# A hybrid layer on one Trainium2 core: the memory rows' sum of squares, computed at another place in the program

## Chip, cores and metric

One core of a Trainium2 chip runs the whole kernel. The metric is device time in microseconds (us) of one execution; the time of a kernel is the median of its runs. Engines are named as in the profile: PE (TensorE matmuls), PEld (its weight loads), DVE (VectorE), ACT (ScalarE), POOL (GpSimd) and SP (SyncE, which here only issues DMAs).

## What is computed

One layer on 256 tokens of width 2048 in float32: a projection to 7,440 columns, a gated delta rule (8 heads) and an RWKV7 recurrence (16 heads) on its parts, an output projection, a cross attention to 256 memory rows, and a squared-ReLU MLP of hidden width 8192. The part that the change touches is the norm of the memory:

```python
def rmsnorm(x, w):
    xf = x.astype(jnp.float32)
    y = xf * lax.rsqrt(jnp.mean(xf * xf, axis=-1, keepdims=True) + RMS_EPS)
    return (y * w.astype(jnp.float32)).astype(x.dtype)
...
    k = (mn @ wk).reshape(b, m, XA_HEADS, XA_HEAD_DIM)
    v = (mn @ wv).reshape(b, m, XA_HEADS, XA_HEAD_DIM)
```

Here mn is rmsnorm(mem). The reciprocal root of each memory row (one number per row, the tile `rm`) is a factor that can be applied behind the matmul, so `rm` is first needed when the projection wk has been accumulated.

## The kernel before

All large products run as split float32: a weight block of 512 KB (`raw`, 128 x 1024) comes in by a DMA of the SP queue, ACT casts a half of it to a high part (`whi`, L239), DVE subtracts to get the low part (`wlo`, L110), and PE runs six matmuls of 512 columns on each half: high by high (L254), high by low (L255), low by high (L257), for two blocks of rows. There are four buffers of `raw` and three each of `whi` and `wlo`. A GEMM of one group of 512 columns takes eight blocks, here called blocks 1 to 8, each with halves a and b.

The input projection is read group by group, `win_group` (L784). The RWKV part takes, for u = 0 to 3, a group with r and k (`rk_group`, L799), for even u a group with v (`v_group`, L804), and then `unit(u)` (L810), the recurrence of four heads. The accumulated group is scaled into two tiles `pt` (128 x 512) of the pool `ptp`, which has four buffers and is also where squares of rows are computed. The delta rule follows (`dn_in`, `dn_unit`), then two groups for its gate (`z_group`), then the memory's projections wk and wv. Each unit inverts a triangular matrix in `inverse` (L481): it writes the matrix to memory (L488), reads the diagonal blocks back as `g16` (L490), works on them with DVE, and goes through memory once more (L519, L521). These four DMAs are issued by ACT.

The sum of squares of the memory rows is `rms_dram` (L292). Eight times, SP issues a load of 128 x 512 of `mem` into a tile `junk` of that pool (L297), and ACT squares it in place and accumulates the row sums (L122, called from L298). DVE then adds the eight sums (L300, L287) and POOL takes the power -0.5 (`rm`, L289). In the kernel before, it is called at L1018, behind `dn_unit(1)` and ahead of the two gate groups.

The program's order is not the order of the code: a scheduler puts each engine's instructions into one list, weight loads and casts first (`high_priority`, L212 and L230), and a list is executed in order. It also decides which buffer of the pool a `junk` tile gets, and so what its load has to wait for.

Of the kernel before, what the change touches and what calls it, by code (L numbers as in the profile page):

```python
# [17 lines left out]
P = 128  # L18
# [86 lines left out]
def body(ctx, tc, I, out, dbg=None, upto=99):  # L105
# [14 lines left out]
    def act(o, a, f, scale=1.0, bias=0.0, accum=None):  # L120
        kw = {} if accum is None else {"accum_out": accum}
        return A.activation(o, a, f, bias=bias, scale=scale, **kw)  # L122
# [16 lines left out]
    def nm(s):  # L139
        cnt[0] += 1  # L140
        return f"{s}_{cnt[0]}"
# [144 lines left out]
    def rms_end(ss, name):  # L286
        ts(ss, ss, 1.0 / D, ALU.mult, EPS, ALU.add)  # L287
        r = const.tile([P, 2], F32, name=name)
        power(r, ss, -0.5, 2)  # L289
        return r  # L290

    def rms_dram(src, name):  # L292
        part = small.tile([P, 2, 4], F32, tag="ssp", name=nm("ssp"))
        for m in range(2):
            for q in range(4):
                junk = ptp.tile([P, 512], F32, tag="pt", name=nm("junk"))
                nc.sync.dma_start(out=junk, in_=src[:, m, 512 * q:512 * (q + 1)])  # L297
                act(junk, junk, AF.Square, accum=part[:, m, q:q + 1])  # L298
        ss = small.tile([P, 2], F32, tag="ss", name=nm("ss"))
        V.tensor_reduce(ss, part, axis=AX.X, op=ALU.add)  # L300
        return rms_end(ss, name)
# [497 lines left out]
    def rk_group(u):  # L799
        pt = win_group()  # L800
        stream[0] = 2
        return rw_shift(pt, 0, ("r", "k"), (2 * u, 2 * u + 1))

    def v_group(u):  # L804
        pt = win_group()
        stream[0] = 2
        for i in range(2):
            vs[u + i] = rw_shift(pt, 256 * i, ("v",), (2 * (u + i), 2 * (u + i) + 1))[0]

    def unit(u, rk_):  # L810
        stream[0] = u % 2
        rw_unit(u, rk_[0], rk_[1], vs[u])

    for u in range(4):
        t = rk_group(u)
        if u % 2 == 0:
            v_group(u)
        unit(u, t)
        if upto <= 1:
            return  # L820
    rps.close()
# [193 lines left out]
    Vm = late.tile([P, 2, NB], F32, name="Vm")  # L1015
    obs = [dn_unit(0, *kqv)]
    obs.append(dn_unit(1, *dn_in(1)))
    rm = rms_dram(I["mem"].rearrange("(m p) d -> p m d", p=P), "rm")  # L1018
    z_group(0)
    z_group(1)  # L1020
    stream[0] = 2
# [217 lines left out]
```

## Time and profile before

| what | value |
|---|---|
| median of 3 runs | 1428.85 us (1423.86 to 1430.27) |
| the profiled execution's own time | 1427.91 us |
| its span, first to last instruction | 1426.2 us |
| PE busy | 1407.6 us, 99% of the span |
| DVE, ACT, POOL busy | 945.7, 776.2, 53.0 us |
| mean granted clock of TensorE | 0.995 |
| DMA traffic | 250.80 MB, 176 GB/s over the span |

The profile is of one execution. Busy time is the time in which an engine had an instruction in work; the row of a wait names the instruction that began late and what came last of the things it waited for. A number in brackets at the end of a timeline row is idle time of that engine ahead of the row. [...]

### The profile page before, as it was taken

The numbers are of one execution on the slowest core, as the hardware profiler recorded it, in microseconds if no ns is written. First come the engines' busy times: TensorE is split into PE (matmuls) and PEld (weight loads), VectorE is DVE, ScalarE is ACT, GpSimd is POOL, SyncE is SP. The second block draws the span as 40 slices with busy tenths as digits, with TensorE's granted clock in tenths as the row PEclk, the third lists the DMA queues.
The fourth block names the chain that finished last, engine by engine and source line by source line (L and its number), as shares of the span: only waits on it lengthen the run. The fifth ranks groups of instructions, "written<-read, shape, count | busy, mean of one in ns | idle before, by whom it ended". The sixth has DMA issues, their size and how long they took to land.

```text
span 1426.2 us, 22860 instructions
## 1 busy us (share of the span) xinstructions
PE 1407.6 (99%) x8308; PEld 1172.1 (82%) x8308; DVE 945.7 (66%) x1788; ACT 776.2 (54%) x1476; POOL 53.0 (4%) x66
## 2 busy tenths in 40 slices
PE   9999999999999999999999999999999999999997
PEld 7877888788887878888788888888888888888886
DVE  7748563858688685766776555665556665566664
ACT  7655554455556454556765544555445544455553
POOL 0010001010010000000000000000000000000000
PEclk9999999999999999999999999999999999999999
DMA  7444443454358455555465566555665556655564
GB/s 272 160 154 142 137 130 106 136 195 140 105 186 238 141 170 173 177 177 178 140 200 189 187 191 198 186 187 192 192 193 191 189 188 194 194 185 188 192 192 148
DMA packets 90114, 250.80 MB, mean 176 GB/s; under 512 B 20609, under 2 KB 29329, under 8 KB 89617
## 3 DMA queue, kind: packets, MB, share of 16 engines
q1 hardware_dynamic: 69728, 241.86, 52.3%
q10 hardware_dynamic: 19920, 6.42, 1.9%
q8 instruction: 65, 1.06, 0.3%
q0 software_dynamic: 352, 1.06, 0.2%
q14 instruction: 49, 0.39, 0.1%
HBM read 242.62 MB, written 6.69 MB: 175 GB/s over the span
## 4 chain that ended last, share of the span: by engine, by line
PE 51%; issue 0%; ACT 0%; DVE 0%; POOLq 0%; POOL 0%
PE ps_g L278 17%; PE ps_g L281 9%; PE ps_g L255 8%; PE ps_g L254 8%; PE ps_g L257 8%; PE ps_g L223 0%; PE ps_g L225 0%; PE ps_g L224 0%; PE ps_x L320 0%; PE ps_s L320 0%; PE ps_s L1112 0%; ACT h L122 0%; ACT junk L122 0%; ACT whi L239 0%; POOLq L1235 0%
## 5 line engine op out<-in xcount | busy, mean ns | idle before, releaser
L110 DVE TENSOR_TENSOR wlo<-raw,whi 128x512 fp32r<-128x512 f32 x848 | 582.1, 691 | 366.6 <-ACT whi L239 314.2
L239 ACT CAST whi<-raw 128x512 fp32r<-128x512 f32 x848 | 524.0, 621 | 485.7 <-DVE wlo L110 202.6
L278 PE MATMUL ps_g<-hhl,whi 128*128 128x512 f32 x1088 | 297.3, 395 | 0.0
L254 PE MATMUL ps_g<-whi,xhl 128*128 128x512 f32 x512 | 207.4, 405 | 0.9 <-ACT whi L239 0.6
L278 PEld LDWEIGHTS ps_g<-hhl,whi 128*128 128x128 f32 x1088 | 186.7, 189 | 25.5
L255 PE MATMUL ps_g<-whi,xhl 128*128 128x512 f32 x512 | 204.1, 399 | 0.0
L254 PE MATMUL ps_g<-whi,fhi 128*128 128x512 f32 x480 | 186.8, 389 | 0.0
L255 PE MATMUL ps_g<-whi,flo 128*128 128x512 f32 x480 | 186.8, 389 | 0.0
L281 PEld LDWEIGHTS ps_g<-hhl,wlo 128*128 128x128 f32 x1088 | 166.3, 189 | 22.6
L281 PE MATMUL ps_g<-hhl,wlo 128*128 128x256 f32 x1088 | 172.9, 281 | 0.0
L257 PE MATMUL ps_g<-wlo,xhl 128*128 128x512 f32 x512 | 170.4, 405 | 2.1 <-DVE wlo L110 2.1
L257 PE MATMUL ps_g<-wlo,fhi 128*128 128x512 f32 x480 | 151.5, 389 | 0.0
L254 PEld LDWEIGHTS ps_g<-whi,xhl 128*128 128x128 f32 x512 | 97.2, 190 | 23.6 <-issue 1.7
L255 PEld LDWEIGHTS ps_g<-whi,xhl 128*128 128x128 f32 x512 | 97.1, 190 | 21.1 <-issue 2.2
L257 PEld LDWEIGHTS ps_g<-wlo,xhl 128*128 128x128 f32 x512 | 94.3, 190 | 23.8 <-DVE wlo L110 4.5
L255 PEld LDWEIGHTS ps_g<-whi,flo 128*128 128x128 f32 x480 | 90.1, 188 | 18.8
L257 PEld LDWEIGHTS ps_g<-wlo,fhi 128*128 128x128 f32 x480 | 90.1, 188 | 18.7
L254 PEld LDWEIGHTS ps_g<-whi,fhi 128*128 128x128 f32 x480 | 90.1, 188 | 18.5
L113 DVE SCALAR_TENSOR_TENSOR cy<-ps_x,colt,cy 128x255 f32<-128x255 f32 (+2 forms) x72 | 34.2, 475 | 2.8 <-ACT cy L122 2.1
L1205 ACT CAST fhi<-hid 128x256 fp32r<-128x256 f32 x64 | 26.1, 407 | 9.7 <-DVE hid L113 9.4
L113 DVE SCALAR_TENSOR_TENSOR h<-ps_g,rf,h 128x512 f32<-128x512 f32 (+1 forms) x34 | 22.9, 716 | 12.0 <-PE ps_g L225 8.7
L113 DVE SCALAR_TENSOR_TENSOR hid<-hid 128x256 f32<-128x256 f32 x64 | 27.3, 427 | 2.1
(353 smaller groups left out, 1440.2 us busy)
## 6 DMA issues: line engine op xcount, KB each, us to landing
raw<-in_w_dram SPq DMA_DIRECT2D x256, 512.0 KB, 4.2
raw<-in_w_in_dram SPq DMA_DIRECT2D x112, 512.0 KB, 3.5
raw<-in_w_out_dram SPq DMA_DIRECT2D x32, 512.0 KB, 4.3
raw<-in_wk_dram SPq DMA_DIRECT2D x8, 512.0 KB, 3.8
raw<-in_wv_dram SPq DMA_DIRECT2D x8, 512.0 KB, 3.5
raw<-in_wq_dram SPq DMA_DIRECT2D x8, 512.0 KB, 3.8
raw<-in_wo_dram SPq DMA_DIRECT2D x8, 512.0 KB, 3.5
wl<-in_w_lora_dram SPq DMA_DIRECT2D x8, 272.0 KB, 6.3
```

The costliest lines, as they stand in the source:

```text
L110: return (e or V).tensor_tensor(o, a, b, op=op)
L113: return V.scalar_tensor_tensor(o, a, s, b, op0=op0, op1=op1)
L239: A.copy(hi, w)
L254: T.matmul(acc[m][:, :n], lhsT=xh, rhs=w[q][0], start=first, stop=False)
L255: T.matmul(acc[m][:, :n], lhsT=xl, rhs=w[q][0], start=False, stop=False)
L257: T.matmul(acc[m][:, :n], lhsT=lhs(kb * KB + q, m)[0], rhs=w[q][1], start=False, stop=last)
L278: T.matmul(acc, lhsT=w[k][0], rhs=rhs(8 * b + k).rearrange("p a t -> p (a t)"), start=b == 0 and k == 0, stop=False)
L281: T.matmul(acc[:, 0:S], lhsT=w[k][1], rhs=rhs(8 * b + k)[:, 0], start=False, stop=b == 1 and k == 7)
L1205: A.copy(hi[:, j], t)
```

## The change

The call of `rms_dram` moves from L1018 to the loop over the RWKV units, behind `unit(1)`. Nothing else is edited.

```diff
@@ -816,6 +816,8 @@
         if u % 2 == 0:
             v_group(u)
         unit(u, t)
+        if u == 1:
+            rm = rms_dram(I["mem"].rearrange("(m p) d -> p m d", p=P), "rm")
         if upto <= 1:
             return
     rps.close()
@@ -1015,7 +1017,6 @@
     Vm = late.tile([P, 2, NB], F32, name="Vm")
     obs = [dn_unit(0, *kqv)]
     obs.append(dn_unit(1, *dn_in(1)))
-    rm = rms_dram(I["mem"].rearrange("(m p) d -> p m d", p=P), "rm")
     z_group(0)
     z_group(1)
     stream[0] = 2
```

What the scheduler makes of it, first on the SP queue, which issues the loads. In the kernel before, the eight loads of the memory (`junk`, numbers 1019 to 1026) stand among the weight loads of the first gate group (its blocks 4 to 8):

```order
L232 DMA raw_1047_5268<-in_w_in_dram 128x1024
L297 DMA junk_1019_5169<-in_mem_dram 128x512
L297 DMA junk_1020_5172<-in_mem_dram 128x512
L232 DMA raw_1052_5290<-in_w_in_dram 128x1024
L297 DMA junk_1021_5175<-in_mem_dram 128x512
L297 DMA junk_1022_5178<-in_mem_dram 128x512
L232 DMA raw_1057_5312<-in_w_in_dram 128x1024
L297 DMA junk_1023_5181<-in_mem_dram 128x512
L232 DMA raw_1062_5334<-in_w_in_dram 128x1024
L297 DMA junk_1024_5184<-in_mem_dram 128x512
```

Now they stand in the fourth group of the input projection, r and k of unit 2 (below: group 4), whose blocks 1 to 8 are `raw_340` to `raw_375` by the first number. The first row is its block 5:

```order
L232 DMA raw_360_1908<-in_w_in_dram 128x1024
L297 DMA junk_327_1787<-in_mem_dram 128x512
L297 DMA junk_328_1790<-in_mem_dram 128x512
L297 DMA junk_329_1793<-in_mem_dram 128x512
L232 DMA raw_365_1930<-in_w_in_dram 128x1024
L297 DMA junk_330_1796<-in_mem_dram 128x512
L232 DMA raw_370_1952<-in_w_in_dram 128x1024
L297 DMA junk_331_1799<-in_mem_dram 128x512
L297 DMA junk_332_1802<-in_mem_dram 128x512
L297 DMA junk_333_1805<-in_mem_dram 128x512
L232 DMA raw_375_1974<-in_w_in_dram 128x1024
L297 DMA junk_334_1808<-in_mem_dram 128x512
```

So all eight loads now go past the loads of blocks 6 to 8 and of the next group. The third to sixth wait, by their semaphores, for the square of the one two places ahead (329 for 327, 330 for 328, 331 for 329, 332 for 330); the seventh and eighth wait for PE's transposes of the `pt` tiles of unit 1.

Second, ACT in group 4, from the cast of half 2b to that of 4b. Before (2b is `whi_338`, 3a `whi_341`, 4b `whi_348`):

```order
L239 CAST whi_338_1818<-raw_335_1812 128x512
L122 ACTIVATE sh_r_255_1381<-ps_x_254_1376,der_81 128x256
L239 CAST whi_341_1836<-raw_340_1834 128x512
L239 CAST whi_343_1840<-raw_340_1834 128x512
L122 ACTIVATE sh_r_255_1381<-ps_x_254_1376,der_81 128x256
L239 CAST whi_346_1858<-raw_345_1856 128x512
L239 CAST whi_348_1862<-raw_345_1856 128x512
```

Now (2b is `whi_348`, 3a `whi_351`, 4b `whi_358`):

```order
L239 CAST whi_348_1848<-raw_345_1842 128x512
L122 ACTIVATE junk_327_1787,ssp_326_1786<-junk_327_1787 128x512
L122 ACTIVATE sh_r_255_1381<-ps_x_254_1376,der_81 128x256
L239 CAST whi_351_1866<-raw_350_1864 128x512
L122 ACTIVATE junk_328_1790,ssp_326_1786<-junk_328_1790 128x512
L239 CAST whi_353_1870<-raw_350_1864 128x512
L122 ACTIVATE sh_r_255_1381<-ps_x_254_1376,der_81 128x256
L239 CAST whi_356_1888<-raw_355_1886 128x512
L122 ACTIVATE junk_329_1793,ssp_326_1786<-junk_329_1793 128x512
L239 CAST whi_358_1892<-raw_355_1886 128x512
```

A square of the memory now stands ahead of the casts of 3a, 3b and 4b, and each square is behind the landing of its load.

Third, ACT around halves 6a and 6b of the same group. Before (6a is `whi_356`, 6b `whi_358`):

```order
L239 CAST whi_353_1884<-raw_350_1878 128x512
L122 ACTIVATE sh_k_257_1391<-ps_x_256_1386,der_81 128x256
L519 DMA inv0_83<-x16_175_935 64x256
L239 CAST whi_356_1902<-raw_355_1900 128x512
L122 ACTIVATE sh_k_257_1391<-ps_x_256_1386,der_81 128x256
L122 ACTIVATE kk_267_1423<-sh_k_257_1391,der_81 128x256
L122 ACTIVATE th_270_1427<-sh_k_257_1391,colt_75 128x256
L239 CAST whi_358_1906<-raw_355_1900 128x512
```

Now (6a is `whi_366`, 6b `whi_368`):

```order
L239 CAST whi_363_1914<-raw_360_1908 128x512
L122 ACTIVATE sh_k_257_1391<-ps_x_256_1386,der_81 128x256
L122 ACTIVATE junk_331_1799,ssp_326_1786<-junk_331_1799 128x512
L519 DMA inv0_83<-x16_175_935 64x256
L239 CAST whi_366_1932<-raw_365_1930 128x512
L122 ACTIVATE junk_332_1802,ssp_326_1786<-junk_332_1802 128x512
L122 ACTIVATE junk_333_1805,ssp_326_1786<-junk_333_1805 128x512
L122 ACTIVATE sh_k_257_1391<-ps_x_256_1386,der_81 128x256
L122 ACTIVATE kk_267_1423<-sh_k_257_1391,der_81 128x256
L122 ACTIVATE th_270_1427<-sh_k_257_1391,colt_75 128x256
L239 CAST whi_368_1936<-raw_365_1930 128x512
```

One square now stands ahead of the cast of 6a, and two more ahead of that of 6b. From group 4 on, up to the memory's projections, the small work of the units also stands elsewhere among the matmuls, by a few places.

## Rows read from the trace of the kernel before

**Rows 1.** The page: busy time by engine, and the chain that ended last.

```profile
PE 1407.6 (99%) x8308; PEld 1172.1 (82%) x8308; DVE 945.7 (66%) x1788; ACT 776.2 (54%) x1476; POOL 53.0 (4%) x66
...
PE 51%; issue 0%; ACT 0%; DVE 0%; POOLq 0%; POOL 0%
```

**Rows 2.** What PE waited for, whole span (total us, times, longest), its second entry.

```profile
PE ps_s L673 <- DVE IP L113: 1.5, 1, 1.5
```

**Rows 3.** Stretches: length, busy PE, PEld, DVE, ACT, POOL (instructions), granted clock, DMA share, GB/s.

```profile
250.00:300.00 50.00, 48.07 (x394) 36.44 (x392) 35.20 (x78) 26.85 (x57) 6.90 (x9) 0.93 0.39 127
...
450.00:500.00 50.00, 49.15 (x436) 38.86 (x435) 36.70 (x87) 27.14 (x52) 5.37 (x3) 0.97 0.51 157
...
272.00:276.00 4.00, 2.49 (x71) 1.68 (x70) 4.00 (x11) 1.24 (x2) 0.00 (x0) 1.00 0.10 25
```

**Rows 4.** The tile junk: durations in ns (min/median/max), starts, waits, time to landing.

```profile
L297 SPq DMA_DIRECT2D junk<-in_mem_dram x8: 328/328/454, 422.4 to 441.3; - x8
L122 ACT ACTIVATE junk<-junk x8: 627/632/634, 428.0 to 445.9; 128x512 f32<-128x512 f32 x8
...
  DMA junk<-in_mem_dram: 4.8, 4
...
DMA to landing us min/median/max: 4.2/4.4/5.1
```

**Rows 5.** What PE waited for between 415 and 455 us.

```profile
PE ps_g L257 <- DVE wlo L110: 1.9, 3, 1.0
```

**Rows 6.** Timelines of ACT, DVE and PE between 427 and 439 us.

```profile
427.97 0.63 ACT L122 ACTIVATE junk<-junk 128x512 f32<-128x512 f32 x1
...
428.60 0.60 ACT L239 CAST whi<-raw 128x512 fp32r<-128x512 f32 x1
...
430.42 0.68 ACTq L490 DMA_DIRECT2D g<-scr  x1
...
437.02 0.17 DVE L117 TENSOR_SCALAR x<-g 64x8 f32<-64x8 f32 x1 [2.83 <-DMA g<-scr]
...
438.44 0.73 PE L257 MATMUL ps_g<-wlo,xhl 128*128 128x512 f32 x2 [1.03 <-DVE wlo L110]
```

**Rows 7.** DMA issues: queue, count, KB each, median us to landing.

```profile
out_dram<-h SPq DMA_DIRECT2D x4, 256.0 KB, 2.9
...
g<-scr ACTq DMA_DIRECT2D x6, 64.0 KB, 3.1
```

**Rows 8.** Timelines of SP and ACT in group 4, 108 to 124 us.

```profile
108.53 0.33 SPq L232 DMA_DIRECT2D raw<-in_w_in_dram  x1
...
111.11 0.62 ACT L239 CAST whi<-raw 128x512 fp32r<-128x512 f32 x1 [2.08 <-PE ps_g L255]
112.01 0.47 ACT L122 ACTIVATE sh_r<-ps_x,der 128x256 f32<-128x256 f32 x1 [0.28 <-PE ps_x L320]
112.38 1.18 ACT L239 CAST whi<-raw 128x512 fp32r<-128x512 f32 x2
...
121.08 0.49 ACTq L519 DMA_DIRECT2D inv<-x  x1
...
122.22 0.47 ACT L122 ACTIVATE sh_k<-ps_x,der 128x256 f32<-128x256 f32 x1
...
123.39 1.13 ACT L239 CAST whi<-raw 128x512 fp32r<-128x512 f32 x2
```

**Rows 9.** Timeline of PE in group 4: the first matmul of halves 3a, 4b, 6a and 6b.

```profile
114.55 0.39 PE L254 MATMUL ps_g<-whi,xhl 128*128 128x512 f32 x1
...
119.19 0.40 PE L254 MATMUL ps_g<-whi,xhl 128*128 128x512 f32 x1
...
123.31 0.39 PE L254 MATMUL ps_g<-whi,xhl 128*128 128x512 f32 x1
...
124.81 0.48 PE L254 MATMUL ps_g<-whi,xhl 128*128 128x512 f32 x1
```

**Rows 10.** What PE waited for between 100 and 160 us.

```profile
PE ps_g L254 <- DVE pt L117: 0.3, 1, 0.3
```

## The prediction

> **What bounds the kernel now.** Read the page's first part and its chain first [rows 1]: PE is busy 1407.6 of 1426.2 us, and the chain that ended last is, where an engine is named at all, PE. DVE (66%) and ACT (54%) have room on the average. So an edit that leaves the matmuls as they are can win only what PE does not use: its waits, and time at the lower clock. Next come the waits of PE over the whole span and the granted clock by stretches [rows 2, 3]. The largest single wait behind the start is 1.5 us; the clock was below 1.00 in two places only: 0.93 over the stretch 250 to 300 and 0.97 over 450 to 500, that is 0.07 x 50 + 0.03 x 50 = 5.0 us of full-speed time lost. Everything that lies on the table is therefore a few us of 1428, and the question is whether the moved step gives or takes such a few us.
>
> **What the step costs where it stands now.** The view of the tile junk [rows 4] shows eight loads of 256 KB issued from 422.4 to 441.3, landing after 4.2 to 5.1 us (median 4.4), and eight squares; ACT stood still 4.8 us in four of them, waiting for the data. PE's waits in that stretch are 1.9 us in three [rows 5]. The longest, 1.03 us at 438.44, can be followed in the timelines [rows 6]: ACT issued the read of the diagonal blocks (g from scr) at 430.42, DVE got it at 437.02 after 2.83 us of standing still, and the low half that PE wanted stood behind it in DVE's list. So this read took 6.6 us, where the median of its six is 3.1 [rows 7]; it ran while the memory's loads did. I count 1.0 us as the step's price there. The other two waits (0.9 us together) are of low halves too; nothing in the rows ties them to the memory, so they are worth between 0 and 0.9. **Given back: 1.0 us, bounds 0 and 1.9.**
>
> **What it costs where it goes.** The work is the same: eight loads, eight squares, two small DVE operations, one POOL operation. A square takes 0.63 us of ACT's list (427.97 to 428.60, [rows 6]), eight of them 5.0. What matters is what stands behind them. In group 4 ACT's casts feed PE with three buffers of high halves, so a cast that is late by more than its lead stops PE. I walk the new lists with the times of the old group 4 [rows 8, 9] and the median landing of 4.4.
>
> Half 3a: the load of block 5 was issued at 108.53; the first memory load follows 0.33 later, 108.9, and lands at 113.3. ACT has finished the cast of 2b at 111.7 and stands. Square until 113.9, the shift sh_r (0.37, from 112.01 to 112.38) until 114.3, then the cast of 3a, 0.62, done at 114.9. PE took up 3a at 114.55. **PE late by 0.4.**
>
> Half 4b: the third load waits for the first square, 114.0, and lands at 118.4; square, cast, done at 119.6. PE was at 4b at 119.19, now 119.6. **Nothing more.** The second square goes into the gap behind the cast of 3a (to 115.5), so the fourth load goes out at 115.5 and lands at 119.9, its square is done at 120.5.
>
> Half 6a: the fifth load waits for the third square, 119.0, lands at 123.4, square to 124.0; ACT issues the DMA L519 (0.49), cast from 124.5, done at 125.1. PE was at 6a at 123.31, with the 0.4 at 123.7. **Late by 1.4.**
>
> Half 6b: the sixth load waits for the fourth square, 120.5, lands at 124.9, the seventh just behind it. Behind the cast of 6a (next start 125.05) come two squares to 126.3, then sh_k, kk and th, 1.17 us as before (122.22 to 123.39), then the cast of 6b, done at 128.1. PE needs it 1.5 us behind 6a (123.31 to 124.81), at 126.6. **Late by 1.5.**
>
> Sum 0.4 + 1.4 + 1.5 = **3.3 us**. With the longest landing of rows 4, 5.1 us, three landings follow each other up to 6a, and the same walk gives 1.1 + 0.7 + 2.1 + 1.5 = 5.4. With the shortest landing for a transfer of this size on this queue, 2.9 us (the output's stores, [rows 7]), only the two squares ahead of 6b are felt, 0.5 us. I take 4.4, because it was measured on these very loads among the same weight loads; 0.5 and 5.4 stay as the ends. The 0.3 us that PE already waited in this part [rows 10] are left as they are.
>
> [...]
>
> **What else moves.** The weight loads that now stand behind memory loads on SP: block 6 is issued behind the third memory load (114.4) and needed by the cast of 6a at 121 or later, so it has 6 us; block 8 is issued behind the seventh (about 121.5) and needed some 6 us behind 6a. Both are covered by a landing of about 4.4 to 5; if that goes to 6, block 8 is late by little. POOL: rm now stands ahead of the eight masks of the next scores, and waits for the last square. That is done before 130; the masks follow matmuls that begin later than that, so I put it at nothing; if a square came 2 us later, the masks would be late by that, off PE's path as long as DVE's inversion has lead. DVE's two small sums (0.15 us each in their place) are nothing beside PE. At the memory's projections rm is simply there.
>
> **The sum.** 3.3 - 1.0 = +2.3 on the profiled execution's own 1427.91 us (span 1426.2, the rest around it): **1430.2 us**. That execution lies 0.9 below the median of the runs shown, 1428.85, so the change against the median is +1.4 to +2.3, a tenth or two of a per cent. 0.5%, about what a measurement of this kernel can tell from no change, is 7.1 us: faster means below 1421.7, slower above 1436.0. I expect no change.
>
> **Rivals.**
>
> *The loads land early.* With 2.9 us instead of 4.4 the cost is 0.5 and the gain stays: 1427.91 + 0.5 - 1.0 = 1427.4. For it: at this place the DMA engines have less to do than between 422 and 446. Against it: here too the weights stream on the same queue, and four of the old squares waited for their data.
>
> *The moved order removes clock falls.* The lower clock at 276 to 288 came just behind a stretch in which PE was busy 2.49 of 4 us [rows 3], among the many tiny matmuls of an inversion, and behind the 1.5 us wait of rows 2. The small work now stands at other places. If both falls (5.0), that wait (1.5) and all of 1.9 us go, and the new place costs 0.5, the sum is -7.9: 1420.0, faster. For it: nothing ties these falls to a fixed place. Against it: six inversions remain, each with its runs of tiny matmuls.
>
> *The new waits bring the lower clock (slower).* Place: halves 6a and 6b of group 4. There PE would stand 2.9 us within 5, or 3.6 with the long landing, as sparse as the 2.49 of 4 us that came ahead of the fall at 276. Price: 5.4 of waits, nothing given back, and a fall such as the one at 276, 0.07 x 50 = 3.5 us: 1427.91 + 8.9 = 1436.8. It decides if the landings are above 5 us and a fall follows; with only one of the two the sum stays within 0.5%. [...] Against it: the 1.03 us wait at 438 was followed by no fall.
>
> **How the numbers follow.** Forecast (no change, near 1430.2) 0.60; loads early (1427.4) 0.22; clock falls gone (1420.0) 0.06; waits plus clock fall (1436.8) 0.12. The first two lie within 0.5%, so faster 0.06, same 0.82, slower 0.12. The range takes in the first two with their bounds. Down: 1427.4 with one of the two falls gone, 3.5, is 1423.9, and single runs of the kernel before go that low, so 1423.5. Up: the waits at 5.4 with a fall, 1436.8, so 1437. Only the faster rival is outside, with what no row shows.
>
> **What would show it.** In the profile of the changed kernel: junk's loads between about 109 and 127 us, its landings near 4.4, ACT idle ahead of the squares until the DMA; PE waits on high halves (ACT L239) of some 3 us between 114 and 130, the largest ahead of 6a and 6b; the read of g in the first delta inversion down to 3 to 5 us and the 1.0 us wait at 438 gone; the clock still falling once or twice behind inversions. I would be wrong if PE shows no new waits there although the landings are above 4 us (then the casts' lead is larger than I read), if the clock drops between 115 and 135, or if waits of several us open somewhere in the units or the delta rule, where I have counted none.

## The result, and the profile after

The changed kernel takes **1442.72 us** (median of 4 runs, 1439.23 to 1446.93), the kernel before beside it 1429.56 (4 runs): ratio **1.0101**, 95% interval 1.0068 to 1.0135. It is slower, by 13 us; no change was forecast, and the time lies outside the range. The profiled execution took 1446.93 us (span 1445.2), 19.0 us more than the profiled one of before.

The page's busy times, which answer to [rows 1]:

```profile
PE 1416.7 (98%) x8308; PEld 1181.5 (82%) x8308; DVE 948.0 (66%) x1788; ACT 777.0 (54%) x1476; POOL 51.4 (4%) x66
```

The same 8308 matmuls keep PE busy 9.1 us longer, and PE stands still 9.9 us longer (28.5 us of the span against 18.6): about half of what was lost is matmuls that run slower. That half is read from the granted clock by stretches (columns as in [rows 3]; the last three are clock, DMA share, GB/s). Before:

```profile
105.00:145.00 40.00, 39.70 (x343) 31.31 (x341) 30.94 (x71) 23.49 (x51) 3.50 (x5) 1.00 0.51 151
145.00:270.00 125.00, 125.00 (x924) 102.67 (x922) 78.11 (x168) 66.67 (x140) 12.45 (x16) 1.00 0.43 129
270.00:310.00 40.00, 38.07 (x371) 28.22 (x371) 22.97 (x47) 21.10 (x47) 5.10 (x8) 0.91 0.46 163
340.00:400.00 60.00, 60.00 (x474) 50.78 (x473) 43.08 (x87) 31.91 (x59) 5.70 (x4) 1.00 0.39 128
400.00:510.00 110.00, 108.07 (x716) 87.04 (x715) 90.37 (x213) 65.69 (x131) 11.76 (x9) 0.98 0.62 192
```

The changed kernel, the same stretches:

```profile
105.00:145.00 40.00, 35.45 (x268) 26.87 (x267) 27.52 (x64) 22.06 (x49) 0.73 (x1) 0.91 0.62 195
145.00:270.00 125.00, 124.36 (x945) 101.50 (x945) 73.64 (x157) 67.34 (x142) 15.88 (x19) 0.99 0.39 119
270.00:310.00 40.00, 37.12 (x339) 28.86 (x338) 27.55 (x58) 19.78 (x44) 3.94 (x6) 0.91 0.42 128
340.00:400.00 60.00, 59.07 (x495) 49.76 (x495) 45.14 (x93) 31.21 (x60) 5.92 (x4) 0.91 0.35 113
400.00:510.00 110.00, 105.59 (x698) 86.95 (x697) 82.56 (x192) 55.59 (x104) 8.96 (x8) 0.97 0.52 159
```

The view gives the granted clock as a share of full speed, so full-speed time lost is (1 - clock) times length, summed: before 3.6 + 2.2 = 5.8 us, after 3.6 + 1.3 + 3.6 + 5.4 + 3.3 = 17.2. So the lower clock took some 11 us of full-speed time. Some of PE's idle time lies in the same stretches, so these 11 and the 9.9 us of idle time overlap and add up to more than 19. Of the idle time, 4.3 us are new waits in group 4 and some 1.4 lie in the first 50 us, ahead of all that the change moves (PE busy 47.41 us there before and 45.98 after); the rest is spread over 145 to 600 us. Two of the stretches with a new loss are the first (group 4, where the loads now stand) and 340 to 400, over 200 us behind the last thing that the diff touches.

What came where it was expected, group 4. The tile junk, against [rows 4]:

```profile
L297 SPq DMA_DIRECT2D junk<-in_mem_dram x8: 327/355/417, 110.7 to 124.1; - x8
L122 ACT ACTIVATE junk<-junk x8: 628/632/634, 115.0 to 131.2; 128x512 f32<-128x512 f32 x8
...
  DMA junk<-in_mem_dram: 5.7, 6
```

What PE waited for between 100 and 160 us, against [rows 10]:

```profile
PE ps_s L659 <- ACT th L122: 2.7, 1, 2.7
PE ps_g L254 <- DVE pt L117: 1.0, 1, 1.0
PE ps_g L257 <- DVE wlo L110: 0.7, 1, 0.7
PE ps_g L254 <- ACT whi L239: 0.2, 1, 0.2
```

The longest one in the timeline, on ACT and then on PE:

```profile
126.99 0.63 ACT L122 ACTIVATE junk<-junk 128x512 f32<-128x512 f32 x1 [1.09 <-DMA junk<-in_mem_dram]
...
128.43 0.63 ACT L122 ACTIVATE junk<-junk 128x512 f32<-128x512 f32 x1 [0.71 <-DMA junk<-in_mem_dram]
...
129.81 0.50 ACT L122 ACTIVATE th<-sh_k,colt 128x256 f32<-128x256 f32 x1
```

```profile
130.36 0.59 PE L659 MATMUL ps_s<-cons,th 128*128 128x2 f32 x2 [2.66 <-ACT th L122]
130.87 0.80 PE L254 MATMUL ps_g<-whi,xhl 128*128 128x512 f32 x1
131.46 0.63 PE L255 MATMUL ps_g<-whi,xhl 128*128 128x512 f32 x1
```

The sixth and seventh square stand on ACT for their loads, th stands behind them, and the small matmuls of L659, which are next on PE, stand for th. (th is a buffer's name; what L659 reads from it here are squares of the unit's k, and not a tanh, as one expectation below has it.) Right behind that wait the granted clock is 0.50 from 131 to 137 us (1.00 up to 130), and a matmul of 512 columns takes 0.63 us where it took 0.40.

What came where nothing was counted, PE at 382 to 390 us:

```profile
381.71 0.40 PE L254 MATMUL ps_g<-whi,xhl 128*128 128x512 f32 x1
381.94 0.95 PE L867 MATMUL ps_s<-cons,sq 128*128 128x1 f32 x8
382.75 0.68 PE L897 MATMUL ps_s<-kq 128*128 128x256 f32 x2
383.27 0.95 PE L867 MATMUL ps_s<-cons,sq 128*128 128x1 f32 x8
384.15 1.14 PE L575 MATMUL ps_s<-Sc,Y 64*64 64x64 f32 x16
385.22 1.10 PE L721 MATMUL ps_s<-vt,Sc 128*128 128x64 f32 x8
386.16 1.63 PE L867 MATMUL ps_s<-cons,sq 128*128 128x1 f32 x8
387.65 1.20 PE L897 MATMUL ps_s<-kq 128*128 128x256 f32 x2
388.65 1.71 PE L867 MATMUL ps_s<-cons,sq 128*128 128x1 f32 x8
390.21 0.77 PE L255 MATMUL ps_g<-whi,xhl 128*128 128x512 f32 x1
```

The same work before (L865 and L895 are the later L867 and L897):

```profile
368.11 1.14 PE L575 MATMUL ps_s<-Sc,Y 64*64 64x64 f32 x16
369.18 1.10 PE L721 MATMUL ps_s<-vt,Sc 128*128 128x64 f32 x8
370.12 0.61 PE L320 MATMUL ps_x<-cons,pt 128*128 128x128 f32 x4
370.48 0.71 PE L257 MATMUL ps_g<-wlo,xhl 128*128 128x512 f32 x2
371.03 0.39 PE L254 MATMUL ps_g<-whi,xhl 128*128 128x512 f32 x1
371.26 0.95 PE L865 MATMUL ps_s<-cons,sq 128*128 128x1 f32 x8
```

In the new order one run of small matmuls follows the other for 8.3 us with no matmul of a projection among them (below: the bunch; L575 is of an inversion, L721 of a unit, L867 and L897 of the delta rule), and inside it the same eight 128 x 1 go from 0.95 us to 1.63 and 1.71; the granted clock is 1.00 up to 386 us and 0.50 from 387 to 396. PE waits for nothing there. This order differs because the scheduler placed the units' and the delta rule's small work anew after the step had moved.

### The profile page after: what moved, and what is told of

Its sections match the earlier page's. It is cut to its first block, busy times and chain, and to the rows that moved or that the text cites. A ratio compares the mean times of both kernels' runs of the same rounds, so it can differ in the third digit from the quotient of the medians.

```text
span 1445.2 us, 22856 instructions
## 1 busy us (share of the span) xinstructions
PE 1416.7 (98%) x8308; PEld 1181.5 (82%) x8308; DVE 948.0 (66%) x1788; ACT 777.0 (54%) x1476; POOL 51.4 (4%) x66
## 4 chain that ended last, share of the span: by engine, by line
PE 50%; issue 0%; ACT 0%; DVE 0%; POOLq 0%; POOL 0%
PE ps_g L278 16%; PE ps_g L281 8%; PE ps_g L255 8%; PE ps_g L254 8%; PE ps_g L257 8%; PE ps_g L223 0%; PE ps_g L225 0%; PE ps_g L224 0%; PE ps_x L320 0%; PE ps_s L320 0%; PE ps_s L1113 0%; ACT h L122 0%; ACT junk L122 0%; ACT whi L239 0%; POOLq L1236 0%
## 5 line engine op out<-in xcount | busy, mean ns | idle before, releaser
L254 PEld LDWEIGHTS ps_g<-whi,fhi 128*128 128x128 f32 x480 | 90.1, 188 | 18.6
```

The source lines that it names most:

```text
L254: T.matmul(acc[m][:, :n], lhsT=xh, rhs=w[q][0], start=first, stop=False)
```

## The experiments

Two of the kernels leave the memory's loads out (and so do not compute the norm of the memory), and one moves the step's call once more. All others keep the computation and the instructions and change only lists, buffers of the loads, or both. Except where the call moves, a helper fixes every engine's list from a table of places.

```diff
         body(ctx, tc, aps, out)
+        pinned(nc, tc)
```

"The old order" is the table taken from the kernel before, "the new order" that of the changed kernel. The measurements first. "Clock" is the median over a kernel's runs of the granted clock over the whole span, and the last columns are the clock of the profiled execution in two stretches. The kernel before ran beside each series of kernels, and its clock is 0.995 in each; the ratio is the recorded one, and the quotient of the medians of a series differs from it by up to 0.1%.

| kernel | us | ratio to before, 95% | clock | 105:145 | 340:400 |
|---|---|---|---|---|---|
| before | 1428.0 to 1429.6 | | 0.995 | 1.00 | 1.00 |
| changed | 1442.72 | 1.0101 (1.0068, 1.0135) | 0.988 | 0.91 | 0.91 |
| old order, new place | 1432.56 | 1.0028 (1.0012, 1.0044) | 0.994 | 0.91 | 1.00 |
| new order, no loads | 1437.38 | 1.0062 (1.0041, 1.0083) | 0.989 | 1.00 | 0.89 |
| old place, no loads | 1427.82 | 0.9983 (0.9968, 0.9998) | 0.994 | 1.00 | 1.00 |
| old order, spread | 1428.58 | 0.9993 (0.9977, 1.0010) | 0.997 | 1.00 | 1.00 |
| old order, late squares | 1436.55 | 1.0056 (1.0039, 1.0074) | 0.992 | 0.91 | 1.00 |
| no wait for inverse | 1434.03 | 1.0032 (1.0015, 1.0048) | 0.993 | 0.91 | 1.00 |
| waits behind casts | 1432.28 | 1.0026 (1.0012, 1.0040) | 0.994 | 0.96 | 0.97 |
| that, and own buffers | 1429.01 | 1.0003 (0.9987, 1.0018) | 0.995 | 0.96 | 0.97 |
| own buffers only | 1432.39 | 1.0024 (1.0013, 1.0035) | 0.994 | 0.96 | 0.97 |
| new order, spread | 1437.79 | 1.0057 (1.0039, 1.0074) | 0.990 | 1.00 | 0.89 |
| the same again | 1436.79 | 1.0052 (1.0033, 1.0071) | 0.991 | 1.00 | 0.91 |
| old order for 340:425 | 1436.35 | 1.0044 (1.0030, 1.0058) | 0.994 | 1.00 | 0.97 |
| old order for 360:400 | 1434.09 | 1.0036 (1.0021, 1.0050) | 0.994 | 1.00 | 1.00 |
| that, and from 450 on | 1432.48 | 1.0031 (1.0020, 1.0043) | 0.996 | 1.00 | 0.97 |
| old order from 450 on | 1438.39 | 1.0065 (1.0047, 1.0084) | 0.990 | 1.00 | 0.91 |
| old order from 340 on | 1432.09 | 1.0024 (1.0011, 1.0037) | 0.993 | 1.00 | 0.94 |
| step behind unit 2 | 1430.75 | 1.0019 (1.0005, 1.0034) | 0.995 | 1.00 | 1.00 |

(The stretches of the row "new order, no loads" are from its second profile.) 0.001 of clock over 1430 us is 1.4 us.

**Place or order.** The first three kernels take the change apart. The old order with the step at its new place:

```diff
-    rm = rms_dram(I["mem"].rearrange("(m p) d -> p m d", p=P), "rm")
...
+        if u == 1:
+            rm = rms_dram(I["mem"].rearrange("(m p) d -> p m d", p=P), "rm")
```

> Every engine's list is written out: all instructions stand in the order of the kernel before, and only the memory's step (8 loads, 8 squares, the two sums, the power) stands in group 4, at the places that it has in the changed kernel's lists. Theory A (two causes): the step's waits in group 4 and the fall of the clock behind them cost about 6 us, and the other 6 to 7 us of the changed kernel come from the new order of the small work. Then this kernel takes 1434 to 1437 us, has the wait of some 2.7 us ahead of the small matmuls of L659 and 1 to 2 us more near it, a fall of the clock near 130 us, and behind group 4 the clock falls of the kernel before (one or two). Theory B (one cause): the late group 4 drags everything behind it; then it takes 1441 to 1444 us. Theory C: the step costs nothing there and all comes from the order; then 1428 to 1431 us.

Measured 1432.56, less than theory A expected and more than theory C, and in its trace between 105 and 145 us:

```profile
105.00:145.00 40.00, 35.02 (x202) 26.18 (x201) 26.37 (x61) 21.11 (x49) 2.21 (x2) 0.91 0.57 177
```

```profile
PE ps_s L659 <- ACT th L122: 3.4, 2, 1.7
```

The new order, and the old place, without the memory's loads:

```diff
-                nc.sync.dma_start(out=junk, in_=src[:, m, 512 * q:512 * (q + 1)])
-                act(junk, junk, AF.Square, accum=part[:, m, q:q + 1])
+                there = cons[:, 0:512]
+                act(junk, there, AF.Square, accum=part[:, m, q:q + 1])
```

> The lists of the changed kernel, written out, but without the eight loads of the memory: the squares stand where they stood and read a constant tile, so they wait for no DMA (the norm of the memory is not computed). Theory A: group 4 loses its waits and the fall near 130 us, and the later falls (about 200, 295, 385, 485 us) stay: 1434 to 1438 us. Theory B (all of it hangs on group 4): 1428 to 1431 us. Theory C (all is order): 1440 to 1444 us.

> The lists of the kernel before, written out, without the eight loads of the memory (the squares read a constant tile; the norm of the memory is not computed): the price that the loads had at the old place. The prediction put the whole step's price there at 1.0 us. The changed kernel's read of g took 6.0 us with no memory load near it, so theory A now says that the price was nothing: 1428 to 1430 us, with the read of g still at 5 us or more and the wait of about 1 us at 438 us still there. If the prediction's reading was right, the read of g falls to about 3 us, the wait is gone, and the time is 1427.5 to 1429.

The new order costs 0.62% with no load in group 4 at all, as theory A expected. Its first profile fell on its fastest execution (1427.53), so it was profiled once more:

> The experiment with the new order and no loads of the memory (squares read a constant tile, so the memory's sum of squares is left out), a second look: its first profile came from its fastest execution (1427.5 us of a median of 1437.4). Theory A: this one's time is 1433 to 1443 us, and what it has over the kernel before lies in falls of the clock between 190 and 480 us, some 15 to 25 us of half clock against 10 before. Rival (the order costs by waits, not by the clock): the falls sum to 10 to 14 us, and the time is lost in waits of VectorE's or ScalarE's work spread over the recurrence.

1433.35 us, and 340 to 400 at 0.89; the same bunch of L867, L897, L575 and L721 stands there from 365.1 to 374.1 us. The median clock, 0.989 against 0.995, is 8.6 us, and the time is 8.7 above before: without loads the order costs mostly clock. Against the old place without loads, which has the same instructions in the old order, it is 9.6 us slower (1437.38 to 1427.82), and the clock (0.989 to 0.994) makes some 7 of them. At the old place the loads cost 0.17% by the recorded ratio (0.02 to 0.32; the medians of that series differ by 0.9 us), with PE's waits for low halves at 0.6 us instead of the 1.9 of [rows 5]; the read of g stayed slow (5.3 us), as theory A expected, and the waits fell, as it did not.

What follows: place alone +0.28%, order alone +0.62%, both +1.01%. Neither is the whole, and their sum is within the interval of the change.

**Why the place costs.** The same step in the same group, but with eight buffers of its own, load k behind the weight load of block k and square k behind that block's casts:

```diff
-                junk = ptp.tile([P, 512], F32, tag="pt", name=nm("junk"))
+                junk = rp.tile([P, 512], F32, tag="junk", bufs=8, name=nm("junk"))
```

```diff
 L232 DMA raw_1820<-in_w_in_dram 128x1024
+L297 DMA junk_1787<-in_mem_dram 128x512
 L232 DMA raw_1842<-in_w_in_dram 128x1024
+L297 DMA junk_1790<-in_mem_dram 128x512
...
 L232 DMA raw_1908<-in_w_in_dram 128x1024
-L297 DMA junk_1787<-in_mem_dram 128x512
-L297 DMA junk_1790<-in_mem_dram 128x512
-L297 DMA junk_1793<-in_mem_dram 128x512
```

> The lists of the kernel before with the step in group 4 again, but spread: the junk tiles have eight buffers of their own, load k of the memory stands behind the load of block k, and square k behind the casts of block k, three blocks later, so that no square waits for its landing. Same loads, same squares, same group. Theory A (what costs is ACT's list standing behind landings): no wait of PE on ACT in group 4, no fall near 130 us, 1428 to 1431 us. Rival (the loads' traffic or ACT's 5 us of work in group 4 costs by itself): 1433 to 1437 us, with PE waits on weight loads or casts there.

1428.58, no difference. That is a balance, though, and not nothing: in its trace group 4 ends 3.6 us later than before (counted by the 384th matmul of the projections), L659 waits 1.3 us once, and the median clock is 0.997, 2.9 us better than before. So theory A's time came, and the fall is gone; a few us of waits, which it did not expect, are not.

To find the link that matters, the old order at the new place was edited once more. Late squares:

```diff
-L122 ACTIVATE junk_1802,ssp_1786<-junk_1802 128x512
-L122 ACTIVATE junk_1805,ssp_1786<-junk_1805 128x512
 L122 ACTIVATE sh_k_1391<-ps_x_1386,der 128x256
 L122 ACTIVATE kk_1423<-sh_k_1391,der 128x256
...
 L521 DMA xc_957<-inv_83 128x8x16
 L239 CAST whi_1954<-raw_1952 128x512
+L122 ACTIVATE junk_1802,ssp_1786<-junk_1802 128x512
+L122 ACTIVATE junk_1805,ssp_1786<-junk_1805 128x512
```

> The kernel with the orders of before and the step at its new place, with one edit: the sixth, seventh and eighth square stand behind the first cast of block 7 of group 4 in ScalarE's order, and not between the casts and copies ahead of it. The loads, their buffers and their places are as in the experiment with the old order and the new place (1432.56 us, 1.0028 of before). Theory A (two causes; here only the first): the cost of the place is the wait of the small matmuls of L659 on a tanh that stands behind squares that wait for their loads, and the fall of the clock behind it; with the late squares off that path the L659 waits are under 1 us in sum between 105 and 150 us, no fall of the clock starts between 110 and 140 us, and the time is 1428 to 1430 us, ratio 0.999 to 1.001. Rival (the loads or their buffers do it, not the squares' place in the list): the block loads and casts of group 4 stay late, the clock falls near 131 us again, and the time stays at 1432 to 1433 us, ratio 1.0025.

Both expectations fell: 1436.55, slower than without the edit (1.0056 against 1.0028). ACT in this trace:

```profile
122.47 0.49 ACTq L519 DMA_DIRECT2D inv<-x  x1
...
124.35 0.50 ACT L122 ACTIVATE th<-sh_k,colt 128x256 f32<-128x256 f32 x1
...
128.55 0.62 ACT L239 CAST whi<-raw 128x512 fp32r<-128x512 f32 x1 [3.20 <-DMA inv<-x]
...
131.33 0.49 ACT L122 ACTIVATE th<-sh_k,colt 128x256 f32<-128x256 f32 x1
```

The first th begins 4 us earlier than with the squares ahead of it (128.26 there), but the second stands behind L521, which waits for a small transfer of the recurrence's inversion, and then behind the three squares that the edit had put there (1.9 us of ACT). That transfer (L519) takes 2.0 us before, and 5.6 here among the loads. PE waits 4.8 us at L659. (The trace is of this kernel's fastest execution, 1431.37 us; what the slower ones lost beyond it, it does not show.) So that wait of ACT was taken away too, L521 behind the second th, and DVE's L494, which waits for the same transfer, behind DVE's work on that half:

```diff
+L122 ACTIVATE kk_1423<-sh_k_1391,der 128x256
+L122 ACTIVATE th_1427<-sh_k_1391,colt 128x256
+L239 CAST whi_1954<-raw_1952 128x512
 L521 DMA xc_957<-inv_83 128x8x16
-L239 CAST whi_1954<-raw_1952 128x512
```

> The experiment with the old order and the late squares (1436.6 us, 1.0056), with two more places changed. Its trace shows ScalarE and VectorE standing 3.2 and 3.5 us for one small transfer of the recurrence's inversion (inv<-x, L519), which took 5.6 us among the loads and 2.0 before: ScalarE at L521, the second half's kk and th behind it, VectorE at L494, the second half's sh_k behind it. Here L521 stands behind that kk and th, and L494 behind VectorE's work of that half. Theory A (in group 4 the cost is th, wherever ScalarE and VectorE stand in front of it): the wait at L659 falls under 1 us, no fall of the clock starts between 110 and 140 us, and the time is 1428 to 1431 us. Rival E (it is the weight loads: block 7 of group 4 is queued on SP behind loads of the memory that wait for buffers, and lands some 5 us late, so PE is short of work whatever th does): PE then waits for block 7's casts instead, the clock falls as before, and the time stays at 1433 to 1437 us.

```profile
PE ps_g L254 <- ACT whi L239: 5.0, 2, 4.6
```

L659 waits for nothing now, and PE waits 4.6 us for a cast instead, as rival E said, but not for its reason. ACT in this trace:

```profile
135.37 0.40 ACT L122 ACTIVATE b<-xc,cons 128x128 f32<-128x128 f32 x1 [2.44 <-DMA xc<-inv]
135.68 1.65 ACT L239 CAST whi<-raw 128x512 fp32r<-128x512 f32 x3
```

The first of these three casts is of half 7b, whose weights had landed at 123.6 (what landed late, at 129.7, is block 8; the expectation has the number wrong). It stood behind b, and b for the inversion's second small transfer (L521), 4.8 us here and 2.2 to 3.0 in the traces up to here. Then the buffers alone, with no list changed:

> The experiment with the old order and the new place (1432.56 us, 1.0028) with eight buffers of their own for the loads, and no place in any list changed: a load of the memory no longer waits for the square of an earlier one, and the weight loads behind it on SP's queue don't either. Rival E (the queue on SP is the cost): block 7's weights are issued within 1 us of before's time, the L659 wait is under 1.5 us, and the time is 1428 to 1430 us. Theory A (th behind squares and behind the slow small transfer): the loads land earlier, but all at once, so the small transfer of the inversion still takes over 4 us, the L659 wait stays over 1.5 us, and the time is 1431 to 1434 us.

1432.39, as without the edit; L659 waits 1.9 us in two, the first small transfer takes 4.7, and the weights in question (block 8) still go out 2.5 us late, at 121.3 against 118.8. Theory A held here. Last, all that waits for a small transfer or a late square stands behind the casts, without and with buffers of its own:

```diff
 L239 CAST whi_1954<-raw_1952 128x512
+L239 CAST whi_1958<-raw_1952 128x512
 L521 DMA xc_957<-inv_83 128x8x16
 L122 ACTIVATE junk_1802,ssp_1786<-junk_1802 128x512
 L122 ACTIVATE junk_1805,ssp_1786<-junk_1805 128x512
+L239 CAST whi_1976<-raw_1974 128x512
+L239 CAST whi_1980<-raw_1974 128x512
 L122 ACTIVATE junk_1808,ssp_1786<-junk_1808 128x512
```

> The last experiment on group 4 (no wait for the inverse, 1434.03 us) moved PE's wait from L659 to a cast. Its trace, read again, shows that this cast, of half 7b, did not wait for its weights (landed at 123.6; what landed late, at 129.7, is block 8) but stood in ScalarE's list behind the copy b from xc, which waited for the inversion's second small transfer (4.8 us there, 2.2 to 3.0 elsewhere). Here all that waits for either transfer or for a late square stands behind the casts of the group: ScalarE's L521 and the sixth and seventh square behind the cast of 7b, the eighth square and b behind the cast of 8b; VectorE's L494, b, its transpose and the two sums of the step behind the low half of 8b. Theory A (in-order lists that stand for small transfers and squares): PE's waits between 105 and 145 us are under 2.5 us in sum, no fall of the clock there (1.00), 1428 to 1431 us. Rival E (block 8's weights, issued late behind the memory's loads, are the next bound): PE waits 2 to 4 us for the casts of block 8, the clock falls, 1433 to 1436 us.

> The same lists, and eight buffers of their own for the memory's loads, so that weights on SP's queue do not stand behind loads that wait for squares. Theory A with E as a second link: under 1.5 us of waits between 105 and 145 us, 1.00 there, 1426 to 1430 us. Rival (the small transfers, 4 to 7 us among the loads, delay the unit itself, so PE waits at the inversion's matmuls L537 instead): a wait of 2 us or more at L537 near 140 us and 1430 to 1434 us.

Lists alone: 1432.28, above theory A's range and below E's. The casts are in time (0.2 us, so E fell), but the waits are 3.6 us and the clock still falls (0.96), and the longest wait is the next one down the list, the inversion's own matmuls:

```profile
PE ps_s L537 <- DVE ss L118: 2.1, 1, 2.1
```

With buffers too that wait is 0.8 us and the time 1429.01, ratio 1.0003 (0.9987 to 1.0018): the place costs nothing that can be measured, although in the trace, which is of the slowest execution (1433.64 us), the small transfers still take 4.0 and 5.3 us, all waits of the stretch sum to 2.8 and the clock falls once (0.96), more than was expected. So no single link carries the cost. Squares that wait for loads stand in ACT's list ahead of th and casts (in the changed kernel ACT stands 5.7 us for them); among the loads the inversion's first small transfer takes 4.0 to 7.0 us, against 2.0 before and 2.0 at the old place without loads, and ACT and DVE stand for it (3.2 and 3.5 us with the late squares); loads that wait for a buffer hold weights up on SP (block 8 goes out at 123.6 us in the changed kernel, at 118.8 before). One mended link shows the next; lists and buffers together, or the spread form, are rid of it.

**Is the order harmless by itself?** The spread form in the new order, twice:

> The orders of the changed kernel, but the loads go to eight buffers of their own, load k behind the weight load of block k of group 4, square k behind the casts of block k (the edit that cost nothing with the orders of before: 0.9993). Theory A (the step's place and the new order of the small work cost time apart from each other): the place costs nothing in this form, the order still costs its part, so 1436 to 1440 us, ratio 1.005 to 1.008, with the falls of the clock between 190 and 480 us still there and none near 130 us. Rival (the order is harmless by itself and costs only when it begins late, behind the delay in group 4): 1428 to 1431 us, ratio 0.999 to 1.002.

> The new order with spread loads once more, on the chip on which its three edits run, so that they are compared with it there. Theory A: as measured first, 1436 to 1440 us, ratio 1.004 to 1.007, with a fall of 10 us or more near 378 us in its trace. Rival (the first measurement was high by chance): 1432 to 1435 us.

1437.79 and 1436.79, ratios 1.0057 and 1.0052, with 1.00 in group 4 and 0.89 and 0.91 from 340 to 400. The order costs its part without any fall in group 4. The step one unit later, in a third order that the scheduler made itself (`if u == 2`):

> The step's call behind the third unit of the recurrence instead of the second, orders as they come out then: the loads stand in the next group of projections, and the small work is in a third order. Theory A: a new order is drawn, so that falls of the clock move; the time may come out anywhere from 1424 to 1445 us, and what it has over or under the kernel before is accounted for by half the difference in microseconds at half clock, plus up to 4 us for waits on squares in the group with the loads. Rival (the cost belongs to group 4, where the projections have the least small work to hide the loads): no group-4 delay, so 1428 to 1431 us whatever the order. Rival (any early place costs the same, as the loads compete with the weights): 1441 to 1444 us.

1.0019 (1.0005, 1.0034), clock as before: a third order does not have this cost. The time alone would also fit the rival by which the cost belongs to group 4; the spread form in the new order, 1.00 there and slow all the same, speaks against that.

**Where in the order.** In the spread form of the new order, a stretch of the program was put into the old order, or all that follows a point of time was. The first two cut at 340 us:

> The experiment with the new order and the spread loads (1437.79 us, 1.0057) in the order of the changed kernel for what starts in its first 340 us, and in the order of before for all that is left then. Theory A (the new order's cost lies in a bunch of small matmuls, L867, L897, L575 and L721, near 372 to 382 us, with hardly a projection matmul among them, and the 13.7 us fall of the clock behind it): 1428 to 1431 us, ratio 0.999 to 1.001, no fall of the clock over 7 us between 340 and 420 us. Rival (the cost is spread over the recurrence, from 150 us on): about half of it stays, 1432 to 1435 us.

> The experiment with the new order and the spread loads (1437.79 us, 1.0057), with one stretch reordered: the 665 instructions (442 on TensorE) that start there between 340 and 425 us stand in the order that they have among themselves in the kernel before; all else is in the changed kernel's order. No instruction, load or buffer differs. Theory A (the bunch of small matmuls in this stretch makes the fall of the clock at 378 us): no fall over 7 us between 340 and 425 us, and the time is 1429 to 1433 us, ratio 1.000 to 1.003. Rival (the falls belong to the new order as a whole and only move): a fall of 10 us or more comes at another place, and the time stays at 1436 to 1439 us.

Neither has the long fall (0.94 and 0.97 over 340 to 400 us, some 7 and 4 us at 0.50), but both opened a wait at the cut (PE at L537 for DVE's b, 3.1 and 2.3 us), and behind the second one matmuls of 512 columns take 0.63 us from 345 to 347, so that their times (1432.09 and 1436.35, both where the rivals had them) tell little of the bunch. At 360 us both orders have done the same work but for two instructions; the edit there, on PE, in short:

```diff
-L867 MATMUL ps_s_768_3874<-cons,sq_3875 128x1 x4
-L897 MATMUL ps_s_780_3927<-kq_3206 128x256
-L867 MATMUL ps_s_768_3874<-cons,sq_3881 128x1 x4
-L575 MATMUL ps_s_596_3106<-Sc_97,Y_3094 64x64 x8
-L721 MATMUL ps_s_598_3117<-vt_2935,Sc_97 128x64 x4
-L867 MATMUL ps_s_768_3874<-cons,sq_3887 128x1 x4
-L897 MATMUL ps_s_780_3927<-kq_3206 128x256
-L867 MATMUL ps_s_768_3874<-cons,sq_3893 128x1 x4
 L255 MATMUL ps_g_4432<-whi_4501,xhl_194 128x512
...
+L254 MATMUL ps_g_4432<-whi_4505,xhl_194 128x512
+L255 MATMUL ps_g_4432<-whi_4505,xhl_194 128x512
+L257 MATMUL ps_g_4431<-wlo_4506,xhl_194 128x512
...
+L867 MATMUL ps_s_768_3874<-cons,sq_3893 128x1 x4
```

> The experiment with the new order and the spread loads (1437.79 us, 1.0057), in which only what starts there between 360 and 400 us (264 instructions, 173 on TensorE) stands in the order of before. The longer stretch tried first (340 to 425 us) took the fall near 378 us away but opened a wait of 2.3 us at its own seam, L537 for b, with a fall at 344 us; at 360 us the two orders have done the same work but for 2 instructions, so that no seam wait should open. Theory A (the bunch of L867, L897, L575 and L721 with hardly a projection between them brings the fall of 13.7 us): no fall over 7 us between 350 and 410 us, 1431 to 1434 us, ratio 1.001 to 1.003. Rival (the new order's cost is not in that bunch): 1436 to 1439 us.

> The edit of the short stretch (360 to 400 us in the order of before), and the order of before again for all that is left at 450 us, where TensorE's lists have done the same work in both. Theory A, extended (the new order costs in two places, the bunch near 378 us, and from 470 to 545 us): 1428 to 1431 us, ratio 0.999 to 1.001. Rival (the order costs a little everywhere): 1432 to 1435 us.

> The new order with spread loads up to 450 us, bunch at 378 us and all, and the order of before for what is left. Theory A, extended: the cost of the bunch stays, that of the later place goes: 1432 to 1435 us, ratio 1.002 to 1.004, with a fall of 10 us or more between 365 and 395 us. Rival (the bunch costs nothing in the end, since its fall only stands in for later ones): 1428 to 1431 us.

The stretch without the edit, in the second spread kernel of the new order, and with it:

```profile
340.00:400.00 60.00, 58.86 (x505) 49.73 (x503) 42.03 (x86) 31.40 (x60) 5.91 (x4) 0.91 0.37 116
```

```profile
340.00:400.00 60.00, 59.08 (x527) 49.45 (x525) 43.88 (x90) 33.00 (x63) 5.70 (x4) 1.00 0.37 121
...
400.00:510.00 110.00, 105.99 (x687) 85.46 (x686) 86.25 (x204) 56.70 (x106) 8.95 (x8) 0.94 0.53 163
```

Reordering 264 instructions takes the fall out of that stretch. All rows of the table together say the same of the stretch, less sharply: the five with the new order there have 0.89 to 0.91 from 340 to 400 us, some 11 to 13 us at 0.50, while of the thirteen with the old order there seven have 1.00, five 0.97 (some 4 us) and one, cut at 340, 0.94. The spread kernel of the new order and the three edits of it that cut at 360 and 450 us ran on one chip: the two without the bunch (13 runs) average 1433.1 us, the two with it (13 runs) 1436.5: 3.4 us, 95% 1.2 to 5.5 (the runs drawn anew 20,000 times). No run without it has a clock below 0.992, nine of the 13 with it have. But the rest of my theory fell: the old order from 450 us on alone saves nothing (1.0065, slower than theory and rival), and the two stretches together stay at 1.0031, as the rival said. In the kernel with the short stretch the next falls are in 400 to 510, at 0.94. About 3 us (1.2 to 5.5) of the new order's cost go with how that one stretch is ordered; the rest is not tied to a place, and its cause stays open beyond this, that most of it is clock.

No kernel here that does the whole work is measurably faster than the one before.

## Why the prediction was wrong

**What bounds the kernel** held: PE, its waits, and its clock. So did the warning that all that is to be had is a few us, as long as the clock stays up; it had not been said that much more is to be lost.

**Group 4, +3.3 us (0.5 to 5.4).** Place and cause held, the end of the walk did not quite. ACT stood for the loads 5.7 us in six; th, which stands ahead of the cast of 6b, came 2.7 us late (1.5 were walked for that half), and casts only 0.2 (1.4 were walked for 6a). PE meets th at L659 before it meets that cast, which the walk left out. With pt (1.0) and a low half (0.7) the waits are 4.6 us, 4.3 more than before, inside the bounds. The median landing was 4.4 us again, but the last two took 5.3 and 6.5, and the weights of block 8 took 6.4, the case that the prediction named as late. One of its signs of being wrong came too: the clock dropped between 115 and 135, at 130.

**Given back, 1.0 us (0 to 1.9).** The term was of the right size as a price and wrong as a refund. Without the loads at all the old place is 0.17% better, some 2.4 us (0.3 to 4.6; 0.9 by the medians). But in the changed kernel the first read of g from scr still takes 6.0 us with no memory load near it:

```profile
457.97 0.17 DVE L117 TENSOR_SCALAR x<-g 64x8 f32<-64x8 f32 x1 [2.75 <-DMA g<-scr]
```

against 2.83 in [rows 6], and PE's waits between 415 and 470 are 1.3 us of low halves. Without loads the same read still takes 5.3. That it was slow because of the memory was an inference from two things at one time.

**What else moves, counted at nothing.** This is the step that failed. It went through the queues and small sums that the step is moved past, and took all that the scheduler places anew as the same work at the same price. The same instructions in the new order cost 0.62% by themselves, most of it in clock; the sum had nothing for that. The prediction had the clue in hand: the first fall of before stood behind a stretch of an inversion's tiny matmuls [rows 3] and a wait of 1.5 us [rows 2], and it used that for a rival in which falls go away and for the price of a fall in group 4, not for new falls elsewhere. (Read by single microseconds that fall lasts from 278 to 285, not 276 to 288; its price, 3.4 us, is near the 3.5 that was used.)

**The rivals.** Slower by waits with a fall of the clock in group 4 was the right mechanism at the right place; its price was 8.9 us, and the trace shows 4.3 of waits and 3.6 of clock. It had 0.12 because a fall was thought to need landings above 5 us; the median was 4.4, and of the two loads whose squares stood ahead of that th one took 4.2 and one 5.3. The DMA engines had less to do in group 4, as the rival of the early landings said (before: share 0.57 from 105 to 124 us, 0.90 from 422 to 446), but the median landing was 4.4 us at both places. The rival of the moved falls had the right cause with the wrong sign. Neither alone gives 13 us; that both could come, and add, was not a case of its own, so the range ended at 1437.

In group 4 the fall follows the longest wait of PE, 2.7 us. The one at 386 follows none: the last wait of PE ahead of it, 0.9 us, ended at 359.6, and PE is busy all of the 9.00 us from 381 to 390.

```profile
381.00:390.00 9.00, 9.00 (x66) 8.56 (x65) 4.86 (x9) 3.21 (x6) 0.00 (x0) 0.80 0.13 50
```

So not every fall here stands behind a wait; what sets one off no run shows.

## What to carry to other kernels

Where a scheduler writes the lists, moving one step is two changes: the step, and a new order of all that was packed around it; pin the order and measure each alone before believing a reason for either. In a kernel bound by PE, a step that waits for a DMA belongs in a list behind everything that PE waits for, with buffers and a queue place that hold nothing else up; with only one of these mended the wait turned up at the next here (4.8 us at L659, then 4.6 for a cast, then 2.1 at L537). And an order is judged by the granted clock too, even where PE never waits: here the clock was 0.89 to 0.91 over 60 us in each of five traces with a run of small matmuls and no large one among them, and 0.94 to 1.00 in the thirteen with the old order there.

## Not expected of the hardware

- A transfer of the inversion (L519, 64 KB, issued by ACT) took 2.0 us before, beside the weight loads of SP, and 4.0 to 7.0 where the memory's loads of 256 KB stood among them.
- The granted clock of the changed kernel was 0.50 from 387 to 396 us with PE busy for 9.00 us of those 9, from within a run of matmuls of 1, 64 and 256 columns (381.9 to 390.2) on, and 1.00 again at 397, among projections. Over 340 to 400 us it was 0.89 to 0.91 in all five traces of the new order in the table; the same work with some projections among it had 1.00 in seven of thirteen, 0.97 in five and 0.94 in one.
- Executions of one kernel differ by clock: of the runs before, one of 1423.83 us had 0.998 and one of 1432.58 us 0.993, and 0.005 of 1426 us is 7.1 of the 8.8 us between them.
